# Sixteen of 22 feed-forward column blocks in the seven-product form instead of ten, six of them prepared in the mixer

## The chip, the cores and the metric

One core of a Trainium2 chip runs the whole program. The metric is device time in microseconds of that core: the median of three runs is 1273.53 (1271.73 to 1273.55).

## The reference

One layer on a sequence of 1024 tokens, 1024 features, fp32. A token mixer (half RWKV-7, half causal convolution) is followed by a feed-forward part. Only the feed-forward part and the order of work at the mixer's end are changed.

```python
def _conv_ffn(h, ffn_up, ffn_conv_w, ffn_conv_b, ffn_down):
    hid = h @ ffn_up                              # 1024 x 1024 by 1024 x 5632
    hid = _causal_dwconv(hid, ffn_conv_w, ffn_conv_b)   # width 3 over tokens
    gate, up = hid[..., :D_FF], hid[..., D_FF:]   # D_FF = 2816 = 22 blocks of 128
    return (gelu(gate) * up) @ ffn_down           # 1024 x 2816 by 2816 x 1024

mix = hybrid_mixer(rms_norm(x)) @ w_out           # the mixer's last step
x = x + rms_norm(mix)
x = x + rms_norm(_conv_ffn(rms_norm(x), ...))
```

## The kernel before

The 1024 tokens are worked in two halves of 512 (half 0 and half 1). Activations lie transposed: features on 128 partitions, 512 tokens along a row. An fp32 product is made as three passes in a faster number format: activation high by weight high, activation low by weight high, activation high by weight low. So every operand has a high half (a cast on ACT) and a low half (operand minus its high half; for weights on POOL, in the down projection on DVE). `weight()` loads a 128 x 512 weight tile `wr` from the SP queue, casts it to `wh` on ACT and subtracts to `wl` on POOL. `wr` has three buffers, `wh` and `wl` have two each, so the next-but-one weight's halves wait until TensorE has used the present ones.

The 22 column blocks of the up projection each have a gate half and an up half. They are made in two ways.

*Plain*: `ffn_pair(h, hs, i, ...)` makes a block for one token half: two projections of 24 matmuls (48 in all), the width-3 convolution (`taps`: on ACT a first tap over the whole tile and three one-column operations for the carry from the half before, on DVE two `scalar_tensor_tensor`), a gelu on ACT and a product on DVE.

*Shared*: a block for both token halves and both branches at once, as a 2 x 2 block product (token half, branch) with seven products in place of eight, 12 matmuls each. Two of the products belong to the gate of half 0 and are made early, in `gates` (24 matmuls; its results are kept in `both[0]` as the gate and `both[1]` as the first product). The other five are made in `shared` (60 matmuls), when half 1's activations exist. They need sums of activations (`S`, made by `act_sums` in twelve parts) and sums of weights. The sums of the up weights of a block are four POOL instructions (`four_sums`, L1056), and the five weight halves it uses are POOL's too. For the first shared block they were made ahead (`usums`).

The down projection `ffn_down` is such a seven-product form over everything; its weight sums (`sums`, eleven groups of four POOL instructions, with loads and stores through DRAM, plus the group for `usums`) are made by the generator `weight_sums`, one group each time `beside` takes from it.

The order of work: at the mixer's end, twelve plain blocks for half 0 (`EARLY = 12`, stored to the DRAM tile `early`) are interleaved with the last of the mixer; then the output projection of half 1 (`w_out`), the norm, `gates` for ten shared blocks (`JOINT = 10`), twelve plain blocks for half 1 (`PLAIN = 12`, stored to `plain`), with activation sums and weight sums beside them, ten shared blocks, and the down projection, ahead of which the stored blocks are loaded back. Within each engine the instructions run in one written order, set when the program is built by a scheduler from priorities (`high_priority`, the streams' `PRIO`) and the `issue_after` marks in `beside`; each engine takes them strictly in that order. All loads and stores are issued from the SP queue.

Of the kernel before, what the change touches and what calls it, by code (L numbers as in the profile page):

```python
# [22 lines left out]
P = 128  # L23
# [31 lines left out]
JOINT = 10  # L55
PLAIN = FT - JOINT

# [41 lines left out]
class Trunk:  # L99
    def __init__(self, ctx, tc, a):  # L100
        self.ctx, self.tc, self.nc, self.a = ctx, tc, tc.nc, a
        self.at = dict(PRIO)
        self.n = 0

        self.low_pool = True

# [57 lines left out]
    def weight(self, src, shape, home=None, held=None, kept=None):  # L164


        with self.tc.high_priority():
            raw = (self.f2p.tile(shape, F32, tag="f2", name=self.nm("wr")) if held is self.hp else
                   self.wp.tile(shape, F32, tag="wr", bufs=3, name=self.nm("wr")))
# [12 lines left out]
        if kept and not kept[0]:  # L182
            self.nc.sync.dma_start(kept[1], lo.bitcast(F32))
        return hi, lo


    def setup(self):
# [19 lines left out]
        self.early = self.dp.tile([EARLY, P, HALF], F32, name="early")  # L207
        self.x1d = self.dp.tile([SEQ, D], F32, name="x1d")
# [72 lines left out]
    def pair(self, what, pool):  # L281
        return tuple(pool.tile([P, HALF], F32R, tag="h", name=self.nm(what)) for _ in range(2))
# [534 lines left out]
    def setup_ffn(self, ctx):  # L817
# [9 lines left out]
        self.ap = pool("actp", 2 * JOINT)  # L827
# [86 lines left out]

    def beside(self, *parts):
# [23 lines left out]
    def gates(self, hs, acts, firsts, side):  # L939
# [128 lines left out]
    def weight_sums(self):  # L1068

        nc, a = self.nc, self.a  # L1070
        work = [(lambda r, c, j=j: a["ffn_down"][c, r * HT + j], lambda n, j=j: self.sums[n - 1, j]) for j in range(HT)]
# [31 lines left out]
    def ffn_down(self, acts):  # L1103
# [4 lines left out]
        B = lambda r, c: lambda j: self.a["ffn_down"][c, r * HT + j]  # L1108
# [53 lines left out]
        def hold(j, every=2):  # L1162

            if j % every == 1 and len(late) < HELD:
                late.append(self.weight(B(1, 1)(HT - HELD + len(late)), [P, 512], held=self.hp))

# [34 lines left out]
    def run(self):  # L1201
# [6 lines left out]
        with ExitStack() as ctx:  # L1208
# [8 lines left out]
            one = [self.ffn_pair(0, h0, i, temp, act()) for i in range(EARLY, PLAIN)]  # L1217
            both = [[act() for _ in range(JOINT)] for _ in range(2)]
# [11 lines left out]
            for n, i in enumerate(range(PLAIN, FT)):  # L1230
                self.shared(i, S, h1[4:], both[0][n], both[1][n], raws[n % 2 * 4:n % 2 * 4 + 4] if n else None)
            kept = []
            for i in range(0, 8, 2):
                two = self.row("row", 4)
                nc.sync.dma_start(two.rearrange("p (i t) -> p i t", i=2), self.early[i:i + 2].rearrange("i p t -> p i t"))
                kept += [two[:, :HALF], two[:, HALF:]]
            back = [self.hp.tile([P, HALF], F32, tag="h", name=self.nm("act")) for _ in range(2 * KT)]
            for i in range(8, EARLY):
                nc.sync.dma_start(back[PLAIN + i - 8], self.early[i])
            for i in range(PLAIN):  # L1240
                nc.sync.dma_start(back[i], self.plain[i])
            acts = [kept + back[PLAIN:] + one + both[0], back[:PLAIN] + both[1]]
            self.ffn_down(acts)

    def mixer(self, sts):
# [222 lines left out]
```

## Time and profile before

| | |
|---|---|
| median of three runs | 1273.53 us |
| the profiled execution | 1273.13 us, its span 1271.4 |
| granted clock of TensorE over the span | 0.99 |
| mixer's last transposes on PE | 623.95 |
| output projection of half 1 starts | 668.09 |
| plain blocks of half 1 start | 776.50 |
| shared blocks start | 911.03 |
| down projection starts | 1051.93 |

A row of the timeline has the start, the duration, the engine, the line, the operation and its tiles, `xN` where N instructions run back to back, and in brackets the idle time before and what ended it. A row of the chain of work that ended last has start, duration, engine, tile, line and count. In group rows the busy time and the mean of one instruction in ns stand behind the bar, then the idle time before them. Tile names are cut of their numbers: `wl` and `wh` are weight halves, `xs`, `pe`, `pb`, `pc` and `Y` are PSUM banks, `b` and `t` raw weights and their sums, `f` and `l` halves of activations, `s` halves of activation sums.

### The profile page before, as it was taken

Reading aid. Unit: us, or ns where it says so; the run is one execution under the profiler, and the core shown is the slowest. Engines: PE = TensorE matmul, PEld = TensorE weight load, DVE = VectorE, ACT = ScalarE, POOL = GpSimd, SP = SyncE. Lnnn points to the kernel's source line nnn. Section 1 sums busy time; section 2 is a strip of 40 time slices with the busy share of each in tenths; the row PEclk is TensorE's granted clock in tenths of the full one; section 3 lists DMA queues with packets and bytes.
Section 4 is the critical chain, followed back from the end, with each engine's and each line's share of the span. In section 5 each row is a group of like instructions: output and inputs, shape, how many; then the busy total and the mean of one; then the engine's idle time right before and its main releaser. Section 6 shows DMA issues by size and latency. Waiting matters only on the chain.

```text
span 1271.4 us, 23025 instructions
## 1 busy us (share of the span) xinstructions
PE 1220.3 (96%) x8460; PEld 990.1 (78%) x8460; DVE 891.2 (70%) x1540; ACT 731.1 (58%) x1518; POOL 495.4 (39%) x438
## 2 busy tenths in 40 slices
PE   6999989999999988999999999999999999999996
PEld 4767767787778877788789878778877888888885
DVE  5286998998679989997631165666356779479667
ACT  7563563655845766566744277776555556545451
POOL 4343320011113332344455369898588860000001
PEclk9999998999999999999999999999999999999999
DMA  7644342343343451232345398888522236336523
GB/s 242 173 133 141 117 134 75 94 134 124 110 135 86 122 183 66 85 84 84 101 132 166 112 336 299 292 305 268 173 65 73 79 127 222 99 98 194 173 76 133
DMA packets 105505, 185.70 MB, mean 146 GB/s; under 512 B 15184, under 2 KB 21712, under 8 KB 105392
## 3 DMA queue, kind: packets, MB, share of 16 engines
q1 hardware_dynamic: 105392, 184.23, 46.2%
q8 instruction: 67, 1.10, 0.4%
q14 instruction: 46, 0.38, 0.1%
HBM read 141.58 MB, written 42.60 MB: 145 GB/s over the span
## 4 chain that ended last, share of the span: by engine, by line
PE 55%; DVE 8%; DMA 3%; POOL 3%; issue 2%; ACT 2%; SPq 0%; POOLq 0%; DVEq 0%; ACTq 0%
PE pb L135 26%; PE pe L135 13%; PE xs L135 11%; PE Y L135 2%; DVE pc L416 2%; PE pc L135 2%; POOL wl L162 1%; DVE nrow L1116 1%; DVE x L1100 1%; POOL b L1056 1%; PE pc L150 1%; DMA pt<-mixd 1%; DMA m<-mixd 1%; PE pe L150 0%; DMA b<-ffn_down 0%
## 5 line engine op out<-in xcount | busy, mean ns | idle before, releaser
L162 POOL TENSOR_TENSOR wl<-wr,wh 128x512 fp32r<-128x512 f32 (+1 forms) x181 | 237.2, 1312 | 247.7 <-ACT wh L162 221.0
L162 ACT CAST wh<-wr 128x512 fp32r<-128x512 f32 (+1 forms) x220 | 135.5, 616 | 170.7 <-issue 43.9
L135 PE MATMUL pb<-h,wh 128*128 128x512 f32 (+3 forms) x720 | 229.5, 398 | 2.5 <-ACT wh L162 1.0
L135 PE MATMUL pb<-f,wh 128*128 128x512 f32 x696 | 219.0, 395 | 2.6 <-ACT wh L162 1.5
L416 DVE SCALAR_TENSOR_TENSOR pc<-c,params,pc 128x512 f32<-128x512 f32 x232 | 174.1, 750 | 8.8 <-ACT pc L413 4.8
L135 PEld LDWEIGHTS pb<-h,wh 128*128 128x128 f32 (+2 forms) x720 | 131.8, 188 | 34.9 <-ACT wh L162 2.6
L135 PEld LDWEIGHTS pb<-f,wh 128*128 128x128 f32 x696 | 130.0, 189 | 31.0 <-ACT wh L162 2.8
L135 PE MATMUL pb<-h,wl 128*128 128x512 f32 (+3 forms) x360 | 146.4, 407 | 2.3 <-POOL wl L162 2.1
L135 PE MATMUL pb<-f,wl 128*128 128x512 f32 x348 | 137.9, 397 | 1.5 <-POOL wl L162 1.5
L157 POOL TENSOR_TENSOR ss<-var,mhalf 128x1 f32<-128x1 f32 x16 | 11.0, 692 | 222.6 <-DVE ss L1097 198.2
L1056 POOL TENSOR_TENSOR b<-b,b 128x512 f32<-128x512 f32 x66 | 86.8, 1317 | 2.8 <-issue 0.9
L135 PE MATMUL pe<-f,wh 128*128 128x512 f32 x272 | 84.2, 391 | 0.1
L135 PEld LDWEIGHTS pb<-h,wl 128*128 128x128 f32 (+2 forms) x360 | 67.7, 188 | 20.7 <-POOL wl L162 4.5
L135 PEld LDWEIGHTS pb<-f,wl 128*128 128x128 f32 x348 | 65.7, 189 | 16.9 <-POOL wl L162 3.1
L135 PE MATMUL xs<-f,wh 128*128 128x512 f32 x200 | 62.0, 391 | 0.4 <-DVE act L953 0.4
L135 PEld LDWEIGHTS pe<-f,wh 128*128 128x128 f32 x272 | 50.9, 188 | 10.6 <-ACT wh L162 0.3
L899 DVE SCALAR_TENSOR_TENSOR pt<-pb,params,pt 128x511 f32<-128x511 f32 (+1 forms) x48 | 35.7, 743 | 30.0 <-ACT ecarry L892 29.5
L162 POOL TENSOR_TENSOR wl<-b,wh 128x512 fp32r<-128x512 f32 x36 | 47.0, 1307 | 21.7 <-ACT wh L162 19.8
L135 PE MATMUL pe<-f,wl 128*128 128x512 f32 x136 | 53.7, 395 | 0.7 <-POOL wl L162 0.7
L706 POOL TENSOR_TENSOR XG<-r,GE 64x256 f32<-64x256 f32 x30 | 20.4, 683 | 86.9 <-DVE r L725 82.0
L178 ACT CAST wh<-wr 128x512 fp32r<-128x512 f32 (+2 forms) x44 | 26.5, 604 | 43.1 <-PE pb L135 31.2
L162 ACT CAST wh<-b 128x512 fp32r<-128x512 f32 x36 | 22.2, 617 | 46.8 <-PE pb L135 18.9
(428 smaller groups left out, 2883.7 us busy)
## 6 DMA issues: line engine op xcount, KB each, us to landing
wr<-ffn_up SPq DMA_DIRECT2D x117, 256.0 KB, 2.8
wr<-w_in SPq DMA_DIRECT2D x80, 256.0 KB, 2.9
b<-ffn_down SPq DMA_DIRECT2D x44, 256.0 KB, 4.4
sums<-b SPq DMA_DIRECT2D x44, 256.0 KB, 4.0
wr<-sums SPq DMA_DIRECT2D x44, 256.0 KB, 2.7
lows<-wl SPq DMA_DIRECT2D x40, 256.0 KB, 3.3
wl<-lows SPq DMA_DIRECT2D x40, 256.0 KB, 2.7
b<-ffn_up SPq DMA_DIRECT2D x40, 256.0 KB, 2.7
```

Source lines behind the costliest of these rows:

```text
L135: return self.nc.tensor.matmul(out, lhsT, rhs, start=start, stop=stop, skip_group_check=skip)
L150: self.nc.tensor.transpose(out, in_, self.con("ident")[:n, :n])
L157: self.nc.gpsimd.tensor_tensor(out, v[:, :n], self.mhalf[:, :n], ALU.pow)
L162: return self.nc.scalar.copy(hi, src), eng.tensor_tensor(lo, src, hi.bitcast(F32), ALU.subtract)
L178: self.nc.scalar.copy(hi, raw)
L416: nc.vector.scalar_tensor_tensor(out, c[:, j:j + HALF], w(j), acc, ALU.mult, ALU.add)
L706: nc.gpsimd.tensor_tensor(x[64:128], R[64:128, gs], w.GE[64:128, c, gs].unsqueeze(2).broadcast_to([64, 4, CH]), ALU.mult)
L899: nc.vector.scalar_tensor_tensor(acc[:, o:], ps[:, :HALF - o], w(j), acc[:, o:], ALU.mult, ALU.add)
L1056: sub = lambda o, x, y, op=ALU.subtract: self.nc.gpsimd.tensor_tensor(o, x, y, op)
L1100: nc.vector.scalar_tensor_tensor(x, f[c], s[:, 1:2], x, ALU.mult, ALU.add)
L1116: nc.vector.tensor_tensor(out, a, b, op)
```

## The change

`JOINT` goes from 10 to 16 and `PLAIN` from 12 to 6. At the mixer's end there are six steps in place of twelve. Each is the new function `ahead`: the early products of one shared block (24 matmuls: first product to the DRAM tile `firsts`, gate to `early`) with one plain block (48). The other ten shared blocks have their early products in `gates` as before. Six plain blocks remain for half 1; each now takes one group of weight sums and two parts of the activation sums. Then four stored pairs are loaded; the sixteen shared blocks run in the order 0, 1, 6 to 15, 2 to 5, and the results of the first two go to DRAM (`stored`), after which the last two stored pairs are loaded. The column blocks enter the down projection in another order (`ORDER`), with its weights indexed to match. Weight sums not yet taken are handed to `ffn_down`, which takes one at every second block of its first product (`rest`). One of the weights held for the last product lies in another pool.

```diff
-JOINT = 10
+JOINT = 16
 PLAIN = FT - JOINT
+AHEAD = EARLY - PLAIN
+STORED = 2
+ORDER = [*range(EARLY, FT), PLAIN + STORED, *range(PLAIN, PLAIN + STORED), *range(PLAIN), *range(PLAIN + STORED + 1, EARLY)]
...
-        self.ap = pool("actp", 2 * JOINT)
+        self.ap = pool("actp", 28)
...
+    def ahead(self, hs, n, row, temp, out):
+        i = PLAIN + n
+        first, gate = row[:, :HALF], row[:, HALF:]
+        accs = [temp() for _ in range(2)]
+        def branch(br):
+            ps = self.project(self.a["ffn_up"][br * FT + n], P, hs)
+            self.taps(0, n, br, ps, accs[br])
+        ps = self.bank()
+        self.four(ps, self.weight(self.a["ffn_up"][i, 0], [P, 4, P]), hs[:4], True, True)
+        with self.tc.high_priority():
+            nc.scalar.copy(first, ps)
+        nc.sync.dma_start(self.firsts[n], first)
+        branch(0)
+        self.four(ps, self.weight(self.a["ffn_up"][i, 1], [P, 4, P]), hs[4:], False, True)
+        self.taps(0, i, 0, ps, gate)
+        nc.scalar.activation(gate, gate, AF.Gelu_apprx_tanh)
+        nc.sync.dma_start(self.early[i], gate)
+        branch(1)
+        nc.scalar.activation(accs[0], accs[0], AF.Gelu_apprx_tanh)
+        nc.vector.tensor_tensor(out, accs[0], accs[1], ALU.mult)
+        nc.sync.dma_start(self.early[n], out)
...
-        product(X, lambda j: A11[j], B(0, 0), True, lambda t: nc.scalar.copy(s1[t], X[t]))
+        def rest(j):
+            if j % 2:
+                next(sums, None)
+        product(X, lambda j: A11[j], B(0, 0), True, lambda t: nc.scalar.copy(s1[t], X[t]), rest)
+        list(sums)
...
             for i in range(PLAIN):
                 nc.sync.dma_start(self.plain[i], self.ffn_pair(1, h1, i, temp))
-                self.beside(sums, *[ss] * (2 if i % 3 == 0 else 1))
+                self.beside(sums, ss, ss)
             list(ss)
-            list(sums)
...
-            for n, i in enumerate(range(PLAIN, FT)):
-                self.shared(i, S, h1[4:], both[0][n], both[1][n], raws[n % 2 * 4:n % 2 * 4 + 4] if n else None)
+            pairs = [fetch(n) for n in range(AHEAD - STORED)]
+            order = [*range(STORED), *range(AHEAD, JOINT), *range(STORED, AHEAD)]
+            for m, n in enumerate(order):
+                two = pairs[n] if n < AHEAD else (both[0][n - AHEAD], both[1][n - AHEAD])
+                self.shared(PLAIN + n, S, h1[4:], *two, raws[m % 2 * 4:m % 2 * 4 + 4] if m else None)
+                if n < STORED:
+                    for h in range(2):
+                        nc.sync.dma_start(self.stored[h, n], two[h])
+                    pairs.append(fetch(AHEAD - STORED + n))
...
-            for i in range(EARLY):
-                if i % 2 == 0:
+            for n in range(PLAIN):
+                if n % 2 == 0:
                     two = self.row("row", 4)
-                nc.sync.dma_start(self.early[i], self.ffn_pair(0, h0, i, piece, two[:, i % 2 * HALF:(i % 2 + 1) * HALF]))
+                self.ahead(h0, n, self.row("row", 4), piece, two[:, n % 2 * HALF:(n % 2 + 1) * HALF])
```

POOL in the first two shared blocks, before. `wl` rows are weight halves (those from `wr_` the first block's, from `b_` and `t_` the second's); L1056 is `four_sums`: its first row of a group makes `t` for a later block, and the three others `b`.

```order
L162 TENSOR_TENSOR wl_10164<-wr_10161,wh_10163 128x512
L162 TENSOR_TENSOR wl_10183<-wr_10180,wh_10182 128x512
L162 TENSOR_TENSOR wl_10203<-wr_10200,wh_10202 128x512
L1056 TENSOR_TENSOR t_1631_10282<-b_10159,b_10157 128x512
L162 TENSOR_TENSOR wl_10222<-wr_10219,wh_10221 128x512
L1056 TENSOR_TENSOR b_10157<-b_10157,b_10156 128x512
L1056 TENSOR_TENSOR t_1648_10401<-b_10155,b_10153 128x512
L1056 TENSOR_TENSOR b_10156<-t_1631_10282,b_10156 128x512
L162 TENSOR_TENSOR wl_10241<-wr_10238,wh_10240 128x512
L1056 TENSOR_TENSOR b_10153<-b_10153,b_10152 128x512
```

The same place after, from the first block's fifth half (`wl_9420`) on. The sums with numbers from 11307 up (`b_11309`, `b_11370` and so on) are those for the down projection; the lines have moved by 34 (L1056 is now L1090).

```order
L167 TENSOR_TENSOR wl_9420<-wr_9417,wh_9419 128x512
L1090 TENSOR_TENSOR b_9320<-b_9320,b_9319 128x512
L1090 TENSOR_TENSOR b_11309<-b_11309,b_11307 128x512
L1090 TENSOR_TENSOR b_9316<-b_9316,b_9315 128x512
L1090 TENSOR_TENSOR b_11370<-b_11370,b_11368 128x512
L1090 TENSOR_TENSOR b_9319<-t_1486_9467,b_9319 128x512
L1090 TENSOR_TENSOR b_9315<-t_1505_9592,b_9315 128x512
L1090 TENSOR_TENSOR b_11368<-b_11368,b_11367 128x512
L1090 TENSOR_TENSOR b_9321<-b_9321,b_9319 128x512
L167 TENSOR_TENSOR wl_9476<-b_9319,wh_9475 128x512
```

In front of the second block's first half (`wl_9476`) there now stand sums for the third block and for the down projection.

DVE at the last plain block and the first shared one, before: taps of the last block, its product, and the first sums of the shared block (`act`, L1013).

```order
L899 SCALAR_TENSOR_TENSOR acc_10142<-pb_10105,params,acc_10142 128x511
L1013 TENSOR_TENSOR act_8164<-act_8164,xs_97 128x512
L899 SCALAR_TENSOR_TENSOR acc_10142<-pb_10105,params,acc_10142 128x510
L912 TENSOR_TENSOR acc_10098<-pb_10061,acc_10142 128x512
L1013 TENSOR_TENSOR acc_10198<-act_8164,xs_98 128x512
```

After: L167 rows into `s` make the low halves of the last activation sums.

```order
L907 SCALAR_TENSOR_TENSOR acc_9277<-pb_9240,params,acc_9277 128x511
L907 SCALAR_TENSOR_TENSOR acc_9277<-pb_9240,params,acc_9277 128x510
L920 TENSOR_TENSOR acc_9233<-pe_9196,acc_9277 128x512
L167 TENSOR_TENSOR s_9177<-pc_9179,s_9177 128x512
L167 TENSOR_TENSOR s_9178<-Y,s_9178 128x512
L1000 TENSOR_TENSOR pb_9307<-f_5989,pb_9307 128x512
L1001 TENSOR_TENSOR pb_9307<-pb_9307,r_9310 128x512
L1047 TENSOR_TENSOR act_9324<-act_9324,xs_99 128x512
```

Behind the last block's product now stand the last two low halves of the activation sums, ahead of the shared block's first sum.

ACT at that place, after: `r` copies and `s` casts belong to the activation sums, `acc` rows to the last plain block.

```order
L167 CAST wh_9361<-wr_9359 128x512
L1016 COPY r_9193<-pe_9180 128x512
L898 ACTIVATE acc_9233<-pe_9196,params 128x512
L898 ACTIVATE acc_9277<-pb_9240,params 128x512
L904 ACTIVATE acc_9233<-ecarry,acc_9233,params 128x1 x2
L167 CAST s_9178<-Y 128x512
L904 ACTIVATE acc_9277<-ecarry,acc_9277,params 128x1 x2
L904 ACTIVATE acc_9233<-ecarry,acc_9233,params 128x1
L904 ACTIVATE acc_9277<-ecarry,acc_9277,params 128x1
L918 ACTIVATE pe_9196<-acc_9233 128x512
```

Before, the last block's first tap was followed directly by its three one-column operations:

```order
L162 CAST wh_10182<-wr_10180 128x512
L890 ACTIVATE acc_10142<-pb_10105,params 128x512
L896 ACTIVATE acc_10142<-ecarry,acc_10142,params 128x1 x3
L162 CAST wh_10202<-wr_10200 128x512
L162 CAST wh_10221<-wr_10219 128x512
```

Copies and casts for the activation sums now lie between them.

More of the change, by code (lines that the diff above doesn't have):

```diff
@@ L167, in weight @@
         with self.tc.high_priority():
-            raw = (self.f2p.tile(shape, F32, tag="f2", name=self.nm("wr")) if held is self.hp else
+            raw = (self.f2p.tile(shape, F32, tag="f2", name=self.nm("wr")) if held and held is not self.h1p else
                    self.wp.tile(shape, F32, tag="wr", bufs=3, name=self.nm("wr")))
@@ L281, in pair @@
     def pair(self, what, pool):
-        return tuple(pool.tile([P, HALF], F32R, tag="h", name=self.nm(what)) for _ in range(2))
+        return tuple(pool.tile([P, HALF], F32R, tag=self.tags.get(pool, "h"), name=self.nm(what)) for _ in range(2))
     def pairs(self, what, pool=None):
@@ L947, in second @@
             self.gated = nc.scalar.activation(act, act, AF.Gelu_apprx_tanh)
-        for n, i in enumerate(range(PLAIN, FT)):
+        for n, i in enumerate(range(EARLY, FT)):
             ps = self.bank()
@@ L1070, in weight_sums @@
         nc, a = self.nc, self.a
-        work = [(lambda r, c, j=j: a["ffn_down"][c, r * HT + j], lambda n, j=j: self.sums[n - 1, j]) for j in range(HT)]
+        work = [(lambda r, c, j=j: a["ffn_down"][c, ORDER[r * HT + j]], lambda n, j=j: self.sums[n - 1, j]) for j in range(HT)]
         work.insert(2, (lambda r, c: a["ffn_up"][c * FT + PLAIN, r].rearrange("p k m -> p (k m)"),
@@ L1164, in hold @@
             if j % every == 1 and len(late) < HELD:
-                late.append(self.weight(B(1, 1)(HT - HELD + len(late)), [P, 512], held=self.hp))
+                home = self.hp if len(late) < HELD - 1 else self.ap
+                late.append(self.weight(B(1, 1)(HT - HELD + len(late)), [P, 512], held=home))
         def after4(j):
@@ L1216, in run @@
             act = lambda: self.ap.tile([P, HALF], F32, tag="act", name=self.nm("act"))
-            one = [self.ffn_pair(0, h0, i, temp, act()) for i in range(EARLY, PLAIN)]
-            both = [[act() for _ in range(JOINT)] for _ in range(2)]
+            both = [[act() for _ in range(FT - EARLY)] for _ in range(2)]
             turn = cycle((True, False))
@@ L1232, in run @@
[L1232 to L1241, printed above, removed]
@@ L1242, in run, with fetch @@
[L1242 to L1243 removed]
+            def fetch(n):
+                pair = act(), act()
+                nc.sync.dma_start(pair[0], self.early[PLAIN + n])
+                nc.sync.dma_start(pair[1], self.firsts[n])
+                return pair
+            pairs = [fetch(n) for n in range(AHEAD - STORED)]
[7 more added lines that the diff above has]
+                    pairs.append(fetch(AHEAD - STORED + n))
@@ new lines, in run @@
+            back = [[self.hp.tile([P, HALF], F32, tag="h", name=self.nm("act")) for _ in range(STORED + PLAIN)] for _ in range(2)]
+            for k in range(STORED + PLAIN):
+                for h in range(2):
+                    src = self.stored[h, k] if k < STORED else (self.plain if h else self.early)[k - STORED]
+                    nc.sync.dma_start(back[h][k], src)
+            acts = [both[h] + [pairs[STORED][h]] + back[h] + [pairs[n][h] for n in range(STORED + 1, AHEAD)] for h in range(2)]
@@ L1245, in mixer @@
+            self.ffn_down(acts, sums)
     def mixer(self, sts):
```

10 lines of the change are left out of this document (7 added, 3 removed).

## The prediction

> **What bounds the kernel now.** I read the page first: busy shares, the slices, and the summary of the chain that ended last.
>
> ```profile
> span 1271.4 us, 23025 instructions
> PE 1220.3 (96%) x8460; PEld 990.1 (78%) x8460; DVE 891.2 (70%) x1540; ACT 731.1 (58%) x1518; POOL 495.4 (39%) x438
> PE   6999989999999988999999999999999999999996
> POOL 4343320011113332344455369898588860000001
> PE 55%; DVE 8%; DMA 3%; POOL 3%; issue 2%; ACT 2%; SPq 0%; POOLq 0%; DVEq 0%; ACTq 0%
> ```
>
> TensorE is the bound nearly everywhere, so a matmul removed is time removed, unless an engine that feeds it falls behind. POOL, 39% over the span, is at eight or nine tenths in slices 25 to 28 and 30 to 32, in the half-1 stages that change. The chain itself gives the price of a matmul and the one place where POOL already releases PE:
>
> ```profile
> 889.43 10.88 PE pe L135 x48
> ...
> 914.47 1.30 POOL wl L162
> ...
> 923.78 2.54 POOL b L1056 x2
> ...
> 928.80 1.72 POOL wl L162
> 930.56 10.76 PE pb L135 x46
> ```
>
> 48 matmuls in 10.88 us are 0.2267 us each. From 914.47 to 930.56, in the first two shared blocks, the chain runs through POOL. The windows give that stage by stage (busy us of PE, PEld, DVE, ACT, POOL; then clock, DMA share, GB/s):
>
> ```profile
> core 0: us, PE busy (x) PEld busy (x) DVE busy (x) ACT busy (x) POOL busy (x), PEclk, DMA share, GB/s
> 776.00:851.00 75.00, 73.67 (x321) 58.98 (x320) 45.30 (x69) 55.61 (x118) 67.26 (x54) 1.00 0.88 297
> 851.00:911.00 60.00, 59.88 (x263) 48.81 (x262) 29.72 (x44) 39.54 (x84) 43.31 (x34) 1.00 0.71 231
> 911.00:941.00 30.00, 28.35 (x121) 22.01 (x120) 14.33 (x21) 14.09 (x29) 25.05 (x20) 1.00 0.34 108
> 941.00:1052.00 111.00, 110.94 (x483) 89.29 (x482) 76.47 (x111) 63.85 (x134) 86.57 (x66) 1.00 0.33 100
> 1052.00:1230.00 178.00, 178.00 (x787) 147.43 (x786) 126.93 (x204) 88.13 (x163) 0.00 (x0) 1.00 0.47 145
> ```
>
> The plain steps of half 1 run at a DMA share of 0.88 and then 0.71, with POOL at 67.26 of 75 us while weight sums are made. The first two shared blocks idle PE, the other eight do not; the down projection never waits. The borders, from PE's timeline, are the first matmul of the plain steps, of the shared stage, of its third block and of the down projection:
>
> ```profile
> 776.50 0.71 PE L135 MATMUL pb<-f,wh 128*128 128x512 f32 x2
> 911.03 0.62 PE L135 MATMUL xs<-s,wh 128*128 128x512 f32 x2
> 941.16 0.61 PE L135 MATMUL xs<-s,wh 128*128 128x512 f32 x2
> 1051.93 0.62 PE L135 MATMUL xs<-wh,a 128*128 128x512 f32 x2
> ```
>
> So before: plain 134.53 us, shared 140.90, of which 30.13 for two blocks and 110.77 for eight, 13.85 each. At 60 x 0.2267 a block is 13.6.
>
> **The change, part by part.** Matmuls by count: 12 mixer steps of 48 become 6 of 72 (-144); 12 plain steps of 48 become 6 (-288); six more shared blocks of 60 (+360). Net -72, or -16.3 us. That is the gain on paper. Each stage then stands as follows.
>
> *Mixer, -32.6.* 144 x 0.2267 = 32.6. The removed matmuls also cover the mixer's own chain, which must reach the output projection in time:
>
> ```profile
> 623.95 0.60 PE L150 MATMUL pc<-const,t 128*128 128x128 f32 x4
> 629.36 2.50 DVE L162 TENSOR_TENSOR l<-co,l 128x512 fp32r<-128x512 f32 x4 [0.56 <-ACT l L162]
> 631.46 0.73 PE L135 MATMUL pb<-f,wh 128*128 128x512 f32 x2 [1.19 <-ACT wh L162]
> 668.09 8.07 PE L135 MATMUL pb<-wm,l 128*128 128x256 f32 x66
> ```
>
> The last low halves of its input end at 631.86 (629.36 + 2.50), and the projection starts at 668.09: 36.2 us of cover for 32.6 removed, so it starts near 635.5 and the cover just holds. Bounds: 0 and +3 (ACT and DVE have the new copies and taps in front of those halves; 1.19 us of PE's idleness there already ends with ACT). I take 0, as the slack is positive. The twelve extra stores and the gate work go under the same PE time.
>
> *Plain steps of half 1, -62.3.* 288 x 0.2267 = 65.3 go. Two things get denser. The activation sums take 12 parts in 6 steps, not in 9. ACT has 55.61 + 39.54 = 95.2 us there; a step's own share is about four weight casts, two first taps, six one-column taps and a gelu, by these rows 4 x 0.62 + 2 x 0.77 + 6 x 0.38 + 0.6 = 6.9:
>
> ```profile
> L162 ACT CAST wh<-wr 128x512 fp32r<-128x512 f32 x48 | 29.9, 622 | 32.1 <-PE pb L135 7.8 <-PE xs L135 7.0 <-issue 5.4
> L896 ACT ACTIVATE acc<-ecarry,acc,params 128x1 f32<-128x1 f32 x69 | 22.8, 384 | 0.3
> L890 ACT ACTIVATE acc<-pb,params 128x512 f32<-128x512 f32 x9 | 7.0, 774 | 0.0
> L910 ACT ACTIVATE pb<-acc 128x512 f32<-128x512 f32 x4 | 2.4, 599 | 1.5 <-DVE acc L899 1.5
> ```
>
> Without six steps 54 us are left in 69, 0.78 against 0.70. I charge +1 (bounds 0 and 5). The eight loads of the four stored pairs are put on the SP queue between the weight loads of the first plain step: 2.1 MB at 297/0.88 = 338 GB/s is 6.2 us of transfers, in the stretch that is fullest already. If all is hidden it costs 0, if none is, 6. I charge +2, nearer the hidden end, since 0.88 leaves 9 us of 75 free, and the stores of the last weight sums move out of this stage.
>
> *Shared stage, +99.1.* This is the term that decides. POOL's instructions run in their written order. At the first shared block they ran like this:
>
> ```profile
> 909.03 1.29 POOL L162 TENSOR_TENSOR wl<-wr,wh 128x512 fp32r<-128x512 f32 x1 [1.43 <-ACT wh L162]
> ...
> 918.79 1.29 POOL L1056 TENSOR_TENSOR b<-b,b 128x512 f32<-128x512 f32 x1
> 920.05 1.29 POOL L1056 TENSOR_TENSOR t<-b,b 128x512 f32<-128x512 f32 x1
> 921.30 1.29 POOL L1056 TENSOR_TENSOR b<-t,b 128x512 f32<-128x512 f32 x1
> 922.55 1.27 POOL L162 TENSOR_TENSOR wl<-wr,wh 128x512 fp32r<-128x512 f32 x1
> ...
> 928.77 1.74 POOL L162 TENSOR_TENSOR wl<-b,wh 128x512 fp32r<-128x512 f32 x1
> ```
>
> The starts 918.79, 920.05, 921.30 and 922.55 are 1.25 to 1.26 us apart: 1.256 per instruction when POOL is behind. The shared stage's first weight half (`wl` at 909.03) starts 2.0 us before its first matmul, call that moment T0. In the new order POOL has 34 instructions from that half up to the one of the third block: 19 of the blocks' own (five halves each for blocks one and two, four sums each for blocks two and three, one sum of block four) and 15 of weight sums for the down projection, since the three that the source hands to that stage are issued here, beside the rest of the one before them. 34 x 1.256 = 42.7, so the third block cannot start before T0 - 2.0 + 42.7 + 0.8 (its half's own 1.29, less two matmuls that don't need it) = T0 + 41.5. Before it was T0 + 30.13.
>
> Weighed against a rule: the Trainium skill, "Perfetto Trace Analysis", section "GPSIMD Engine Instruction", says that POOL spans are unreliable and that start-to-start spacing is the thing to count. The rows agree (1.29 reported, 1.256 apart). By reported spans the 34 would take 43.9 us, and the sum would come out 1.2 us higher.
>
> A second delay comes before it. The activation sum that the first shared product multiplies is finished late: by the new order on DVE its last low halves stand behind the four taps and the product of the last plain step. Before, these ran at
>
> ```profile
> 913.08 0.75 DVE L899 SCALAR_TENSOR_TENSOR acc<-pb,params,acc 128x511 f32<-128x511 f32 x1 [3.90 <-DMA b<-ffn_up]
> 914.56 0.74 DVE L899 SCALAR_TENSOR_TENSOR acc<-pb,params,acc 128x510 f32<-128x510 f32 x1
> 915.40 0.69 DVE L912 TENSOR_TENSOR acc<-pb,acc 128x512 f32<-128x512 f32 x1
> ```
>
> so the product ended at T0 + 5.1. Two low halves of 0.6 behind it and the three matmuls that use them end the first shared product at T0 + 7.0. ACT now also has a copy, a second first tap, a cast and three more one-column taps in that place, 0.6 + 0.77 + 0.6 + 3 x 0.38 = 3.1 (an estimate from ACT's rows above, a copy or cast of this width put at 0.6), which makes it T0 + 10.1. Weight halves have two buffers, so POOL's third half waits until the first product is done; it stands seventh in the 34 and would come at T0 + 5.5. The chain slips by 1.5 to 4.6, or by 0 if the sums are done in time; I take 4.6, since the order puts all of those ACT rows in front. After the third block POOL has nine instructions per block, 11.3 us of 13.6, and stops binding; 14 x 13.85 = 193.9. The stage: 41.5 + 4.6 + 193.9 = 240.0 against 140.9. Without either delay it would be 30.1 + 193.9 = 224.0, +83.1.
>
> *Down projection, 0.* Permuting blocks changes addresses, not counts. The sixteen loads that bring stored activations back stand ahead of a few weight loads, with a DMA share of 0.33 before them: 0 to +2. A weight held in another pool costs nothing, the instructions being the same. The late weight sums land long before the product that reads them.
>
> Sum: -32.6 - 62.3 + 99.1 + 0 = +4.2. The profiled run took 1273.13 us, 1.7 more than its span, which stays; so 1277.3. The median of the runs is 0.4 above that run: **1277.7 us**. What a measurement of this kernel can tell from no change is about 0.2%, 2.5 us.
>
> **The rivals.** *Sums ready in time* (faster): if the scheduler's placing of ACT and DVE work leaves the activation sums done before T0 + 5.5, the 4.6 goes; if the plain stage then hides its loads and copies, 3 more go: 1277.7 - 7.6 = 1270.1. Place: the first product of the shared stage. It decides at 6.7 us recovered, 2.5 below the median of before; for it speaks DVE at 29.72 of 60 us before, against it the order. *One of the two charges goes* (no change): 1273 to 1275, since they are worth 3 and 4.6, and the other stays. *POOL's backlog is absorbed* (faster by much): the 34 do not bind, +83.1 holds, 1257 to 1261. That needs weight sums to have run ahead of T0, which an in-order queue whose halves wait for PE's buffers does not allow; 43.31 us of POOL in 60 before says there is room, not that the order uses it. *The mixer's cover is gone and the loads are not hidden* (slower still): +3 and +4 on top, 1281 to 1286; for it speaks 36.2 against 32.6.
>
> The second rule: the Trainium skill, "SBUF — State Buffer", section "Who interferes with whom", says that a DVE instruction with two SBUF inputs contends with a GpSimd one that reads SBUF. The trace agrees: the `wl` at 928.77 took 1.74 us, not 1.29, beside
>
> ```profile
> 927.94 1.41 DVE L1048 TENSOR_TENSOR act<-act,acc 128x512 f32<-128x512 f32 x1
> ```
>
> Two blocks lie in the backlog, so by that rule the sum would be 2 x 0.45 = 0.9 us more, within the forecast's own range.
>
> **How the numbers follow.** Forecast 0.43, own range 1274 to 1283; slower still 0.11; one charge goes 0.22; sums in time 0.17; backlog absorbed 0.07. Slower is the first two, 0.53 after a little is taken for the forecast's lower edge; same 0.22 and that 0.01; faster 0.24. The range leaves out 0.1 above and the absorbed case below: 1267 to 1287.
>
> **What would show it.** PE's output projection at 633 to 638; the plain stage near 72 us; POOL without a gap for some 45 us from just before the first shared matmul, with weight-sum instructions between the blocks' own; PE idle 15 us or more in the first two shared blocks with POOL `wl` as the releaser, then 13.85 per block; no wait in the down projection. Wrong if the third block starts within 35 us of the first (the POOL count is not what binds), if the output projection waits more than 3 us, or if later shared blocks wait.

## Result and the profile after

The changed kernel takes 1283.47 us (median of four runs, 1282.45 to 1284.83) against 1273.54 before: ratio 1.0075, 95% interval 1.0062 to 1.0087. That is 9.9 us slower, where 4.2 was forecast. The profiled execution took 1284.83 us, 1.4 above the median. The page, with the rows that answer to those of before:

```profile
span 1283.1 us, 22908 instructions
PE 1215.2 (95%) x8388; PEld 979.9 (76%) x8388; DVE 912.6 (71%) x1570; ACT 728.2 (57%) x1516; POOL 517.9 (40%) x456
PE   6989999999999989999999999869999999999997
POOL 4343320011113332344452698798888860000001
PE 45%; DVE 11%; DMA 6%; POOL 5%; issue 3%; ACT 3%; SPq 0%; POOLq 0%; DVEq 0%; ACTq 0%
```

PE's busy time fell by 5 us where 72 matmuls (16.3 us) went, and its row now has an 8 and a 6 in slices 26 and 27, where it had nines. TensorE's share of the chain that ended last fell from 55% to 45%; DVE, DMA and POOL took most of it. The borders of the stages, from PE's timeline (output projection, plain steps, shared stage, its third block, down projection):

```profile
640.82 1.43 PE L140 MATMUL pb<-wm,l 128*128 128x256 f32 x10
749.59 0.71 PE L140 MATMUL pb<-f,wh 128*128 128x512 f32 x2
820.12 0.62 PE L140 MATMUL xs<-s,wh 128*128 128x512 f32 x2
867.37 0.61 PE L140 MATMUL xs<-s,wh 128*128 128x512 f32 x2
1063.20 0.62 PE L140 MATMUL xs<-wh,a 128*128 128x512 f32 x2
```

| stage | before, us | forecast | after, us | change |
|---|---|---|---|---|
| start to output projection | 668.09 | -32.6 | 640.82 | -27.3 |
| output projection and gates | 108.41 | 0 | 108.77 | +0.4 |
| plain steps of half 1 | 134.53 | -62.3 | 70.53 | -64.0 |
| first two shared blocks | 30.13 | +16.0 | 47.25 | +17.1 |
| the other shared blocks (8, then 14) | 110.77 | +83.1 | 195.83 | +85.1 |
| down projection to the end | 219.47 | 0 | 219.90 | +0.4 |

The sum is +11.7 in these two executions. The windows of the changed stages:

```profile
749.59:820.12 70.53, 67.46 (x292) 53.61 (x290) 47.00 (x72) 54.42 (x113) 61.52 (x49) 1.00 0.91 324
820.12:867.37 47.25, 33.96 (x121) 24.79 (x120) 19.12 (x28) 17.63 (x36) 42.35 (x35) 0.86 0.72 252
867.37:1063.20 195.83, 194.53 (x842) 155.77 (x840) 132.47 (x189) 109.09 (x232) 158.32 (x120) 1.00 0.28 84
```

In the second row POOL works 42.35 of 47.25 us and PE only 33.96. PE's waits there, in the order of the timeline:

```profile
828.25 0.80 PE L140 MATMUL xs<-s,wh 128*128 128x512 f32 x1 [3.08 <-DVE s L167]
838.88 0.50 PE L140 MATMUL pe<-f,wl 128*128 128x512 f32 x1 [1.73 <-POOL wl L167]
846.15 1.22 PE L140 MATMUL pe<-s,wh 128*128 128x512 f32 x2 [4.69 <-ACT wh L167]
850.40 0.79 PE L140 MATMUL pe<-s,wl 128*128 128x512 f32 x1 [2.17 <-POOL wl L167]
850.99 1.05 PE L140 MATMUL pe<-s,wh 128*128 128x512 f32 x2
```

First it waits for the low half `s` of the late activation sum, then for weight halves. POOL has one pause there, which the prediction did not have: its sixth instruction waits for a transfer of the late weight sums. From then on it runs without a gap; the rows are that first instruction and some later pieces of the run:

```profile
828.85 1.28 POOL L1090 TENSOR_TENSOR b<-b,b 128x512 f32<-128x512 f32 x1 [3.46 <-DMA sums<-b]
838.77 5.45 POOL L1090 TENSOR_TENSOR b<-b,b 128x512 f32<-128x512 f32 x4
844.19 2.49 POOL L1090 TENSOR_TENSOR b<-t,b 128x512 f32<-128x512 f32 x2
846.63 2.50 POOL L1090 TENSOR_TENSOR b<-b,b 128x512 f32<-128x512 f32 x2
849.09 2.50 POOL L167 TENSOR_TENSOR wl<-b,wh 128x512 fp32r<-128x512 f32 x2
851.54 5.00 POOL L1090 TENSOR_TENSOR b<-b,b 128x512 f32<-128x512 f32 x4
```

Eight sums stand in front of the second block's first two halves (`wl`): its own, some of the third block's, and some for the down projection. That is the queue that the prediction counted: from 828.85 on, 28 instructions take 35.1 us, 1.255 each. PE's wait of 4.69 us belongs to it as well, since the cast that ended it had itself waited for one of the sums. The pause cost little: the next weight half (830.08) needed ACT's cast of 829.13, done at 829.75, and would have come about 0.3 us sooner without it (an estimate from these times).

Two matmuls took 1.05 us at 850.99, against 0.61 at 867.37, and the granted clock over the stretch was 0.86: after its long waits PE was also slow. The Trainium skill, "TensorE: Matmul & The Clock Gate", section "What's actually happening", says that the clock is halved after a window of idleness; the rows behind the wait of 4.69 us agree. Behind the shorter wait of 3.08 us the matmuls were slow as well: they start 0.43 us apart at 829.27, against 0.23 at full clock.

### The profile page after: what moved, and what is told of

Read it like the earlier page. It is cut to its first block, busy times and chain, and to the rows that moved or that the text cites. A ratio compares the mean times of both kernels' runs of the same rounds, so it can differ in the third digit from the quotient of the medians.

```text
span 1283.1 us, 22908 instructions
## 1 busy us (share of the span) xinstructions
PE 1215.2 (95%) x8388; PEld 979.9 (76%) x8388; DVE 912.6 (71%) x1570; ACT 728.2 (57%) x1516; POOL 517.9 (40%) x456
## 4 chain that ended last, share of the span: by engine, by line
PE 45%; DVE 11%; DMA 6%; POOL 5%; issue 3%; ACT 3%; SPq 0%; POOLq 0%; DVEq 0%; ACTq 0%
PE pb L140 20%; PE pe L140 11%; PE xs L140 9%; POOL wl L167 3%; DVE pc L423 2%; PE Y L140 2%; POOL b L1090 2%; PE pc L140 2%; DMA b<-ffn_up 1%; DMA sums<-b 1%; DMA act<-early 1%; DVE nrow L1150 1%; DVE x L1134 1%; DMA pt<-mixd 1%; DMA x1d<-nrow 1%
## 5 line engine op out<-in xcount | busy, mean ns | idle before, releaser
L167 POOL TENSOR_TENSOR wl<-wr,wh 128x512 fp32r<-128x512 f32 (+1 forms) x145 | 188.9, 1304 | 219.9 <-ACT wh L167 190.9
L140 PE MATMUL pb<-f,wh 128*128 128x512 f32 x592 | 188.0, 398 | 3.9 <-DVE pt L907 1.7
L167 ACT CAST wh<-wr 128x512 fp32r<-128x512 f32 (+1 forms) x184 | 113.0, 615 | 130.0 <-issue 36.3
L140 PEld LDWEIGHTS pb<-f,wh 128*128 128x128 f32 x592 | 109.9, 189 | 28.9 <-ACT wh L167 3.8
L140 PE MATMUL pb<-f,wl 128*128 128x512 f32 x296 | 117.7, 398 | 2.4 <-POOL wl L167 2.4
L1090 POOL TENSOR_TENSOR b<-b,b 128x512 f32<-128x512 f32 x78 | 104.2, 1341 | 7.0 <-DMA sums<-b 3.5
L167 POOL TENSOR_TENSOR wl<-b,wh 128x512 fp32r<-128x512 f32 x60 | 77.9, 1299 | 31.5 <-ACT wh L167 29.4
L167 ACT CAST wh<-b 128x512 fp32r<-128x512 f32 x60 | 37.0, 618 | 81.6 <-PE pb L140 34.4
L167 DVE TENSOR_TENSOR a<-act,a 128x512 fp32r<-128x512 f32 x66 | 44.6, 693 | 22.9 <-ACT a L167 20.6
L167 ACT CAST a<-act 128x512 fp32r<-128x512 f32 x66 | 39.5, 618 | 37.3 <-PE Y L140 20.5
L140 PEld LDWEIGHTS pe<-f,wh 128*128 128x128 f32 x256 | 48.1, 189 | 10.1 <-ACT wh L167 0.5
```

The source lines that it names most:

```text
L140: return self.nc.tensor.matmul(out, lhsT, rhs, start=start, stop=stop, skip_group_check=skip)
L167: return self.nc.scalar.copy(hi, src), eng.tensor_tensor(lo, src, hi.bitcast(F32), ALU.subtract)
L1090: sub = lambda o, x, y, op=ALU.subtract: self.nc.gpsimd.tensor_tensor(o, x, y, op)
```

## The experiments

Two theories stood after this. A: POOL's queue and the late activation sums set the first two blocks, as predicted. B: only one of them matters, or something else (loads). The first four runs take each away by itself, take both away, and add POOL's work to the kernel before. T0 is again the first matmul of the shared stage.

**Late weight sums moved into the down projection**

```diff
+        mark = self.low
         def rest(j):
             if j % 2:
-                next(sums, None)
+                with self.tc.issue_after(mark.ins):
+                    next(sums, None)
```

> The changed kernel with one edit: the last three groups of weight sums may not be issued before the last shared block's POOL work is issued, so they run in the down projection. By the order POOL then has 23 instructions, not 34, from the first shared product's weight half to that of the third block. Theory A (POOL's count and the late activation sums set the stage): the first product still ends near T0 + 10, the other 108 matmuls of two blocks take 24.5, the third block starts at T0 + 34.5 to 36 instead of 47.25, and the time falls by 11 to 13 us, to about 1271.5. Rival B (the activation sums alone are the cause, POOL only waits for them): 1281 to 1283. Rival C (the sums only move and hold up the down projection): 1280 or more, with PE waits behind 1063.

Measured: 1287.02 us, ratio to before 1.0100 (1.0082 to 1.0118). The stage did what theory A says, a little short of it: the third block starts 37.43 us after the first, 9.8 less than in the changed kernel, and the down projection starts at 1055.34, not 1063.20. But that projection then took 229.9 us, not 219.9: rival C holds for the total. In its first product, the timelines of PE, of DVE and of POOL:

```profile
1066.95 0.80 PE L140 MATMUL xs<-wl,a 128*128 128x512 f32 x1 [6.51 <-DVE wl L167]
```

```profile
1055.93 6.84 DVE L1150 TENSOR_TENSOR s<-act,act 128x512 f32<-128x512 f32 x4
```

```profile
1052.46 13.10 POOL L1090 TENSOR_TENSOR b<-b,b 128x512 f32<-128x512 f32 x8
```

The same DVE work in the changed kernel:

```profile
1062.19 2.49 DVE L1150 TENSOR_TENSOR s<-act,act 128x512 f32<-128x512 f32 x4
```

Four DVE subtractions with both inputs in SBUF took 6.84 us beside POOL's sums, 2.49 without. PE waited 6.51 us for a weight half that stood behind them on DVE. The sums had left one queue to stand in the way of another engine.

**Activation sums taken earlier**

```diff
-                self.beside(sums, ss, ss)
+                self.beside(sums, *[ss] * (3 if i < 4 else 0))
```

> The changed kernel with one edit: the twelve parts of the activation sums are taken three per plain step in the first four steps, not two per step in six; the weight sums stay where they are. Theory A: the first product no longer waits for a low half of a sum, but POOL still has 32 instructions to the third block, which starts near T0 + 39: 8 us less than 47.25, 1275.5, if nothing else holds POOL; if the loads of the late weight sums hold it until T0 + 8.7 as now, only 2 to 3 us less, 1280.5. Rival B (the late activation sums are the whole cause): 17 us less, 1266. Denser sums on ACT could give back 1 to 3 us in the plain steps.

Measured: 1294.14 us, 1.0162 (1.0140 to 1.0185). It misses every case. The plain steps took 79.6 us, 9 more, with PE waiting behind ACT's copies for the sums:

```profile
787.79 0.74 PE L140 MATMUL pb<-f,wh 128*128 128x512 f32 x2 [1.50 <-ACT r L1016]
794.91 0.73 PE L140 MATMUL pb<-f,wh 128*128 128x512 f32 x2 [1.35 <-DVE f L167]
803.01 0.73 PE L140 MATMUL pe<-f,wh 128*128 128x512 f32 x2 [2.35 <-ACT r L1016]
```

The first product now ran through in 6.3 us (10.0 before the edit), yet the third block started at T0 + 45.5, not 39. Rival B is out: it asked for 17 us less, and with early sums but POOL's full queue the stage got 1.8 us shorter. Why 45.5 and not 39 is told further down.

**Both edits** (the two diffs above together)

> The changed kernel with both edits: activation sums three parts per step in the first four plain steps, and the last three groups of weight sums in the down projection. 22 POOL instructions to the third block. Theory A: the third block starts at T0 + 28 to 30, 17 to 19 us less than the changed kernel: 1265 to 1267, 0.6% below the kernel before. Rival D (loads of stored pairs and raw weights on the SP queue set the start of the stage): the stage keeps more than 8 us of stall, 1273 or more.

Measured: 1288.43 us, 1.0106 (1.0087 to 1.0126). The total missed, since both costs came along: 7.4 us in the plain steps and 10 in the down projection. The stage itself came nearer than in either: third block at T0 + 33.55 (827.15 to 860.70), 13.7 less. Rival D, a stage held by loads, asked for more than 8 us of stall; it kept 6.4 over 27.2 of matmuls, so it is not shown; what held the stage for these 6.4 us was not taken apart.

**The kernel before, with its weight sums late**

```diff
-                self.beside(sums, *[ss] * (2 if i % 3 == 0 else 1))
+                self.beside(*[sums] * (i >= 6), *[ss] * (2 if i % 3 == 0 else 1))
...
-            list(sums)
...
-            self.ffn_down(acts)
+            self.ffn_down(acts, sums)
```

`ffn_down` takes the rest of the sums in its first product, as in the changed kernel.

> The kernel before, with the weight sums alone moved: none in the first six of the twelve plain steps, one group in each of the last six, the last three groups handed to the down projection as in the changed kernel. By the order their instructions then stand between those of the first shared blocks, 31 from the first half to the third block's, while the activation sums are ready early. Theory A (POOL's count): third block at T0 + 37.7 instead of 30.1, 7.6 us more, 1281. Rival B (activation sums are the cause): within 1.5 us of the kernel before, 1273.5.

Measured: 1287.63 us, 1.0114 (1.0092 to 1.0137). The third block is 38.44 us behind the first, against 37.7 forecast by count:

```profile
911.27 0.61 PE L135 MATMUL xs<-s,wh 128*128 128x512 f32 x2
949.71 1.47 PE L135 MATMUL xs<-s,wh 128*128 128x512 f32 x4
```

The two blocks behind it lost another 5.1 us (33.1 against 28.0), which the count to the third block did not cover, so the total missed its 1281. POOL waited for transfers only 0.3 us in these two blocks, so here it is the queue and not the loads. No stored pair, no mixer change and no late activation sum is in this kernel: POOL's sums alone, put at this place, cost more than the whole change does.

**Late weight sums spread over the shared blocks**

```diff
+            if self.fine:
+                yield
+                for n, t, x, y, op in (...):
+                    nc.gpsimd.tensor_tensor(b[t], b[x], b[y], op)
+                    nc.sync.dma_start(dst(n), b[t])
+                    yield
+                continue
...
+                self.fine = True
+                if m:
+                    with self.tc.issue_after(self.low.ins):
+                        next(sums, None)
```

The first step of a group issues its loads; each further one issues one of the four sums, behind one shared block.

> The changed kernel with one edit: the last three groups of weight sums are issued one POOL instruction per shared block, from the third block on, their loads a block ahead. POOL has 23 instructions to the third block as with the sums in the down projection, and ten per block after it (12.6 us of 13.85). Theory A (POOL's queue at the start of the stage): the third block starts at T0 + 37 to 38 as with the sums in the down projection, the later blocks keep 13.9 each, and the down projection gets back the 10 us it lost there beside POOL: 1273 to 1275. Rival (the sums cost what they cost wherever they stand, since POOL and DVE slow each other): 0.5 us or more per later block, 1280 or more.

Measured: 1274.99 us, 1.0010 (0.9999 to 1.0022), as forecast: the third block at T0 + 37.65 (816.11 to 853.76), the later blocks 13.95 each, the down projection with 0.6 us of waits. The same sums, with the same POOL instructions, cost 8.5 us less here than where the changed kernel has them.

**The mixer's copy on DVE, and 48 matmuls left out**

```diff
-            nc.scalar.copy(first, ps)
+            nc.vector.tensor_copy(first, ps)
```

> The changed kernel with one edit: in the six mixer steps the copy of the first product is made by DVE, not ACT. If ACT's queue in front of the output projection's halves is what takes the mixer's missing gain (27.3 us measured, 32.6 counted), the output projection starts 1 to 2 us earlier and the time falls to 1281.5 to 1282.5; if it is spread over clock and single waits, no change, 1283.5.

Measured: 1285.22 us, 1.0090 (1.0073 to 1.0107). The output projection started at 638.96, 1.9 earlier, but the whole was not faster. Nor is the 1.9 shown to be the copy's: the seven kernels with the copy on ACT started it anywhere from 636.87 to 641.28, and the later one with this copy on DVE at 640.39.

> The changed kernel with 48 matmuls left out in the mixer: the plain blocks of the last two mixer steps multiply only the first half of the features (4 x 12 matmuls and 4 weights less; the output is not the reference's). PE-bound theory: 10.9 us less, 1272.6. If the mixer's own chain has used up the cover (its last input was ready at 638.65, the projection started at 640.82), only 2 to 4 us less, 1279.5 to 1281.5, with PE idle ahead of the output projection.

> The same left out of the kernel before: the last two plain blocks of the mixer multiply only the first half of the features (48 matmuls and 4 weights less; the output is not the reference's). There 36 us of matmuls stood between the chain's last input and the output projection, so both theories give the full 10.9 us less: 1262.6.

Both kernels leave out half of the features in two plain blocks, so their output is not the layer's. The edit of the second; in the first it stands in `ahead`'s `branch`, for its last two steps:

```diff
-            pss.append(self.project(self.a["ffn_up"][br * FT + i], P, hs))
+            if h or i not in (EARLY - 2, EARLY - 1):
+                pss.append(self.project(self.a["ffn_up"][br * FT + i], P, hs))
+            else:
+                pss.append(self.bank())
+                self.four(pss[br], self.weight(self.a["ffn_up"][br * FT + i, 0], [P, 4, P]), hs[:4], True, True)
```

The kernel before took 1265.58 us, 0.9930 (0.9914 to 0.9947); its output projection started at 660.44 instead of 668.09, with no wait for its inputs (7.7 us, not 10.9; the clock was 0.87 from 440 to 480 us there, 0.96 without the edit). The changed one took 1291.58, 1.0135 (1.0120 to 1.0150). Its output projection waited for its inputs:

```profile
631.96 0.76 PE L155 MATMUL pc<-const,t 128*128 128x128 f32 x4 [2.27 <-DVE t L439]
636.17 1.22 PE L140 MATMUL pb<-wm,l 128*128 128x256 f32 x4 [3.45 <-ACT l L167]
```

So the cover is nearly used up after the change, as the margin of 36.2 us against 32.6 said: with 48 more matmuls removed the projection started 4.7 us earlier, not 10.9, and PE waited 5.7 us for its chain. Even the kernel before, with ample cover, gained 7.7 for these 48 and not 10.9. The rest of the changed kernel's loss here, and that of the one with the copy on DVE, came in the shared stage (52.4 and 50.1 us for two blocks), though neither edit touches it. The reason stands in DVE's timeline, here of the kernel with the copy on DVE:

```profile
843.14 12.00 DVE L1082 TENSOR_TENSOR act<-act,acc 128x512 f32<-128x512 f32 x1
```

and in POOL's beside it:

```profile
843.48 3.72 POOL L1090 TENSOR_TENSOR b<-b,b 128x512 f32<-128x512 f32 x3
847.15 2.50 POOL L167 TENSOR_TENSOR wl<-b,wh 128x512 fp32r<-128x512 f32 x2
849.60 4.98 POOL L1090 TENSOR_TENSOR b<-b,b 128x512 f32<-128x512 f32 x4
857.89 1.28 POOL L167 TENSOR_TENSOR wl<-t,wh 128x512 fp32r<-128x512 f32 x1 [3.30 <-ACT wh L167]
```

One product of two SBUF tiles, 0.7 to 1.8 us in the other blocks, ended 12.00 us after its start, 0.56 us after POOL first had a gap (its run ended at 854.58). The kernel with 48 matmuls less shows 11.85 us for the same instruction, and the one with early activation sums 6.00, which can account for much of its 6.5 us over the count: ACT then stood idle for 6.31 us until DVE went on, and PE for 6.78 us until ACT did. In the changed kernel it took 0.83, beside a run of POOL as dense, and the four POOL sums there took 5.45 us, not 5.00; why it got its turn is open. The next run takes away the second SBUF input.

**The same product read from PSUM**

```diff
         self.taps(0, i, 1, y, two[0])
-        nc.vector.tensor_tensor(act0, act0, two[0], ALU.mult)
+        nc.scalar.copy(y, two[0])
+        nc.vector.tensor_tensor(act0, act0, y, ALU.mult)
```

> The kernel with the first product's copy on DVE (1285.2), with one more edit: in the shared blocks ACT copies the convolved up part to a PSUM bank and DVE's product with the gate reads it from there, so that this DVE instruction has one SBUF input instead of two. In the kernel without it, that product took 12.00 us in the second shared block, while POOL ran 14 instructions without a pause, and PE idled 4.2 and then 1.9 us behind it. Theory L (a DVE instruction with two SBUF inputs is kept out as long as POOL runs without a pause): the product takes 0.7 us in every block, the first two blocks take 46 to 48 us instead of 50.1, the time falls to 1281 to 1283. Rival (that product only waited for something the profile does not show): it still takes more than 2 us in the second block; 1285 or more with 0.6 us of ACT work added to each block.

Measured: 1284.09 us, 1.0080 (1.0053 to 1.0107). The total is too uncertain to tell it from 1285.22. The instruction is not:

```profile
848.56 0.69 DVE L1083 TENSOR_TENSOR act<-act,xs 128x512 f32<-128x512 f32 x1 [1.43 <-ACT xs L1082]
```

0.69 us beside as unbroken a run of POOL, and never more in the 16 blocks, where the form with two SBUF inputs varied from 0.68 to 1.8 us in every kernel apart from the three long ones; the first two blocks took 47.59, not 50.10. This fits theory L for the instruction, and its rival is out for this execution. As the changed kernel escaped with two SBUF inputs, one execution does not prove the long case cured. It was worth about 2.5 us of this stage, not the 4 of PE's waits, since POOL's queue stays.

**Activation sums a little earlier, weight sums spread**

The edit goes on top of the kernel with spread sums.

```diff
-                self.beside(sums, ss, ss)
+                self.beside(sums, *[ss] * (3, 2, 2, 2, 2, 1)[i])
```

> The kernel with the late weight sums spread over the shared blocks (1275.0), with the twelve parts of the activation sums taken 3, 2, 2, 2, 2, 1 per plain step, not 2 in each. If the late activation sums (first product 10.6 us long, not 2.7) are most of what is left in the first two blocks (37.7 us against 27.2 of matmuls), they fall to 30 to 34, and the plain steps lose 0 to 3: 1269 to 1273. If the denser start costs the plain steps as much as three parts per step did (7.4 us), 1277 or more.

Measured: 1269.87 us, 0.9965 (0.9953 to 0.9978): 0.35% faster than the kernel before and 13.6 us faster than the changed one. The windows of its plain steps and first two shared blocks:

```profile
749.70:820.65 70.95, 67.83 (x292) 53.47 (x290) 46.90 (x73) 53.02 (x112) 61.47 (x49) 1.00 0.90 317
820.65:853.21 32.56, 29.65 (x122) 21.75 (x120) 19.55 (x30) 18.50 (x39) 27.83 (x23) 1.00 0.67 237
```

The plain steps kept their time (70.95), and the two blocks took 32.56 us instead of 47.25, at full clock.

**The first block's third product first**

> That kernel (parts 3, 2, 2, 2, 2, 1 and late weight sums spread), with the first shared block's third product multiplied first: it needs the activation sum that is ready earliest. Theory (activation sums still late): another 1 to 2.7 us less than without it. Rival (POOL's and ACT's weight halves set the first block, not the sums): no change or up to 2 us more.

```diff
+        if raws is None:
+            self.four(z, T(3), S[3], True, True)
         self.four(x, T(2), S[2], True, True)
...
-        self.four(z, T(3), S[3], True, True)
+        if raws is not None:
+            self.four(z, T(3), S[3], True, True)
```

Measured: 1270.29 us, 0.9977 (0.9962 to 0.9993); not to be told from the run without it. The third block came 2.0 us sooner (T0 + 30.56), but the first product waited 1.91 us for ACT's weight half, ahead of T0; nothing was gained.

## Why the prediction was right, and where not

Direction, place and mechanism held; the size did not. The change was 9.9 us against 4.2: inside the outer range (1267 to 1287), but 0.5 us above the forecast's own (1274 to 1283), in the band of the rival *slower still* (1281 to 1286). In the profiled executions the terms missed by +5.3 (mixer), +0.4, -1.7 (plain steps), +3.1 (shared stage) and +0.4.

*Shared stage, forecast +99.1, measured +102.2.* The step that decided the sign holds: where POOL's queue is long, its count gives the third block within 1.2 us (34 instructions and late activation sums: T0 + 47.25, forecast 46.1; 31 and early ones, in the kernel before: 38.44, forecast 37.7), and taking the late sums out of it gives most of the loss back. With 23 and late sums (37.43 and 37.65) and with 22 and early ones (33.55 and 32.56) the count no longer binds: 37.43 and 33.55 are 1.4 and 3.6 us over the latest times that were expected by it, and what held the blocks there was not taken apart. The kernel with 32 and early ones came at 45.49, with DVE held up. The second delay came out at its size: the first product was forecast to end at T0 + 10.1, and its successor started at 830.13, T0 + 10.0, for the reason given, the `s` halves behind the last step's taps:

```profile
825.28 1.52 DVE L907 SCALAR_TENSOR_TENSOR acc<-pb,params,acc 128x511 f32<-128x511 f32 x2
826.91 0.69 DVE L920 TENSOR_TENSOR acc<-pe,acc 128x512 f32<-128x512 f32 x1
827.52 0.68 DVE L167 TENSOR_TENSOR s<-pc,s 128x512 fp32r<-128x512 f32 x1
828.11 0.68 DVE L167 TENSOR_TENSOR s<-Y,s 128x512 fp32r<-128x512 f32 x1
```

The 0.1 us of agreement is in part luck: the last plain product was done at T0 + 7.5, where 3.1 us of extra ACT work had put it at 8.2, and the last matmuls took 1.3 us behind PE's wait, not 0.7. In the two blocks PE stood idle 13.3 us, not the 15 or more that was to be seen, about 9 of them behind POOL's queue. What the forecast did not have is PE's slow clock behind the waits, and 0.14 us more per later block (13.99 against 13.85), 1.9 in all.

*Mixer, forecast -32.6, measured -27.3: the mis-sized term, outside its bounds of 0 and +3.* The projection started at 640.82, not at 633 to 638. That the cover just holds was taken as the full gain. It did hold: the last input was ready at 638.65 and PE went from its matmuls to the projection at 640.82 without a wait. But the chain came 6.8 us later than before (631.86), 1.75 of it in its last step on DVE, where four halves had taken 2.50 us. POOL made weight halves beside them here; that this is why was not tested:

```profile
634.40 4.25 DVE L167 TENSOR_TENSOR l<-co,l 128x512 fp32r<-128x512 f32 x4 [0.90 <-ACT l L167]
```

And the matmuls ahead did not shrink by their full price. PE had 1.9 us more of idle time ahead of the projection, and 1.5 us were lost before 311 us, in code that did not change, where the clock was 0.93 from 100 to 200 us against 0.97. The rest stays open. It is not this one execution: the six other kernels with this mixer started the projection at 636.87 to 641.28, none at the forecast 635.5.

*Plain steps, forecast -62.3, measured -64.0.* The 3 us charged for denser copies and for the loads of stored pairs cost 1.3, at a DMA share of 0.91. The run with three parts per step shows the reserve was small: 9 us more.

*Down projection, forecast 0, measured +0.4.*

*The rivals.* "Sums ready in time" named a real lever of the wrong size alone: early activation sums without relief of POOL gained 1.8 us in the stage (in an execution that also held up DVE for 6 us), and with relief 5.1 (37.65 to 32.56). "One of the two charges goes" was out by its number; its half on the plain steps came true for the larger part (1.3 us of the 3 charged). "POOL's backlog is absorbed" was out, as argued. "Slower still" has the number, and half of its mechanism: the mixer fell short, by more than its +3, but the loads of the stored pairs were nearly hidden; in place of their +4 came the 3.1 of the shared stage. The rule of the Trainium skill, "SBUF — State Buffer", section "Who interferes with whom", was weighed at 0.9 us for POOL's side. In the kernels of the experiments the cost lay on DVE's side: 6.84 us against 2.49 in the down projection, and 12.00 us against 0.69 in the shared stage. The changed kernel itself escaped these two.

## What to carry to other kernels

Count the instructions that stand in an in-order queue between two points, times their spacing, before believing a mean load: POOL was 40% busy and still held PE for some 9 us at one border of stages. Work called late in the source is not late if it is issued at high priority; look where the order puts it, and give it out one instruction at a time where the queue has slack. A removed matmul is worth its time only as long as no chain behind it needed the cover.

## What the runs showed of the hardware

A DVE instruction with both inputs in SBUF was held up for as long as POOL ran two-input instructions without a pause: 12.00, 11.85 and 6.00 us for an instruction of 0.7, each ending about 0.55 us after POOL's run did. With one of its inputs in PSUM it took 0.69 us in the same place. In the down projection the two took turns instead (1.7 us each), and in the changed kernel the same instruction took 0.83; what decides between turns and exclusion stays open. And PE's matmuls ran at about half speed for some 9 us behind a wait of 4.69 us (1.05 us for a pair, 0.61 else).
